# A hybrid decoder block on one core: root of the norms on ScalarE, other loads and order around the second norm

## The chip, the core and the metric

The kernel runs on one core of a Trainium2 chip. Its engines work side by side, each through its own instructions in order: TensorE (PE, matmuls; PEld are its weight loads), VectorE (DVE), ScalarE (ACT), GpSimd (POOL), and SyncE (SP), which here only issues loads. The metric is device time in microseconds (us), the median of several runs; lower is better. All times of the trace count from the first instruction of one profiled execution.

## What is computed

One block for a sequence of 256 positions of width 2048, all in float32 (cut):

```python
mod = silu(c) @ w_mod + b_mod                     # 6 x 2048 columns
sh1, sc1, g1, sh2, sc2, g2 = split(mod, 6)
h = rms_norm(x, norm1_g) * (1 + sc1) + sh1
q, k, v, u, gates = split(h @ w_in)
...                                               # attention, state space branch
x = x + g1 * (merged @ w_out)
h2 = rms_norm(x, norm2_g) * (1 + sc2) + sh2
val, gt = split(causal_dwconv(h2 @ w_up, conv_w, conv_b))
x = x + g2 * ((silu(gt) * val) @ w_down)

def rms_norm(x, g):
    return x * rsqrt(mean(x * x) + EPS) * g
```

## The kernel before

Activations lie with channels on the 128 partitions and the 256 positions along the row. Every weight is streamed once from memory in tiles of 128 x 1024 float32 (512 KB). A float32 product is made of three faster products: ScalarE rounds a weight tile to `whi` (`split_hi`, line 213), VectorE takes the rest, `wlo` = tile - whi (`split_lo`, line 218), and the activations are split in the same way into a pair hi and lo. `raw`, the ring of loaded weight tiles, has five buffers (RAW), `whi` and `wlo` three each (WB); a tile gives its `raw` buffer back when both splits have read it.

The program writes a list, `plan`, of weight tiles and modulation tiles. `go` walks it: `split_ahead(n)` splits up to the tile two behind the current one, `load_ahead` issues loads (line 143, on SyncE's queue) as far as the rings have room, then the tile's matmuls are written. Modulation tiles ("m" entries) are woven between the weights. Two kinds exist: `mod_block` multiplies a tile on TensorE by the conditioning vector (`modp`, line 491, tile matmuls of 512 columns that appear as two records each), copies the sums (`rows`, line 498) and transposes them into columns (`cols_of`, `modt`, line 514); `gate_block` multiplies and sums a tile on VectorE (line 529). After the state space branch the modulation tiles have a ring of their own, `mraw`, with four buffers (MRAW).

A scheduler then fixes the order of the instructions of each engine. It takes the dependencies, the order in which they were written as priority, and its own estimate of when an instruction could start; so a load that waits for nothing can go far ahead of its place in the program. Two devices steer it. `after(a, b)` is an edge that only orders a behind b. And a modulation load into `mraw` is held back by a one-column copy on VectorE from the latest `wlo` into the buffer to be loaded (line 141): the load cannot start before that split.

The stage around the change: the w_out projection (`outp`, blocks b = 0 to 7, 32 weight tiles), whose last block adds each half into x at once (`add_to`, line 356) and squares it on ScalarE (`squares`, line 564; sums over channels by matmuls `sqs`, line 569); `norm_rows(st2)`; the late modulation tiles, the last LATE = 4 units of two tiles each, which give the shift columns 12 to 15 of sh2; then `up_pair(0, 0)`, the first products of w_up (`gp`, then `vp`). `norm_rows` copies the sums, transposes them by two matmuls (`pv`), computes 1/sqrt with a bit trick and three Newton steps on VectorE (`rsqrt`, lines 431 to 435, ten operations on 128 x 2), and spreads the result over all partitions through a diagonal matrix (`dg`) and two matmuls (`pr`) into `rb`. `modulate(c, ...)` then makes the pair `HL[c]`: t = x * a * rb on VectorE (line 603), hi = t + shift on ScalarE (line 607), lo on VectorE (line 608). The first FIRST = 2 pairs are made before the products start, the other six one for each weight step (`spread`). `HL[c]` lies in buffer hl`c`; hl4 to hl7 hold the gated branch (`yg`) until the products `ppp` have read it.

The order of writing here is: w_out's products, `norm_rows`, late tiles, three splits of the next weights (`split_ahead(done["hi"])`), two modulations, then the products. `follow` puts the first weight matmul behind the last modulation matmul.

## Time and profile before

| | |
|---|---|
| runs shown | 1523.32, 1524.7, 1530.68 us; median 1524.7 |
| the profiled execution | 1520.47 us, of which the span from the first to the last instruction is 1518.6 |
| busy | PE 1463.7 us (96%), PEld 1237.9 (82%), DVE 1109.5 (73%), ACT 842.0 (55%), POOL 9.8 (1%) |
| loads | 353.47 MB, mean 233 GB/s |
| mean granted TensorE clock | 0.987 of 2.4 GHz |

Busy times of different engines overlap, so their sum says nothing; what sets the end is the chain of waits. A matmul's row can be longer than the distance to the next one, since they are pipelined: distances between starts are the rate.

### The profile page before, as it was taken

To read this page: it belongs to the slowest core of one execution; us is meant where nothing else is said; L and a number is where in the kernel's file an instruction comes from. 1 tells how busy PE (TensorE), PEld (TensorE's weight loads), DVE (VectorE), ACT (ScalarE), POOL (GpSimd) and SP (SyncE) were. 2 spreads that over 40 slices of the span, in tenths; PEclk is the share of its full clock that TensorE was granted. 3 is DMA by queue.
4 is the path that set the end of the run, shared out by engine and by line. 5 is a ranking of instruction groups with operands and counts; after the bars stand their busy time and mean duration, and the time that the engine had idled before them with its cause. 6 is when DMAs were issued, how large, how long until landed. Compare 5 with 4: busy or idle time off the path is not lost.

```text
span 1518.6 us, 24307 instructions
## 1 busy us (share of the span) xinstructions
PE 1463.7 (96%) x9382; PEld 1237.9 (82%) x9382; DVE 1109.5 (73%) x1881; ACT 842.0 (55%) x1193; POOL 9.8 (1%) x22
## 2 busy tenths in 40 slices
PE   7979999899999999999989999999999999999998
PEld 4657768689977788888868888888888888888887
DVE  3879865886677889998578888886555667766654
ACT  4755767867775534654445555555444455555443
POOL 1000000000000000000000000000000000000000
PEclk9989999999999999999999999999999999999999
DMA  8878888533458887978576777775555555555663
GB/s 322 306 238 307 304 321 296 179 126 126 139 170 298 300 301 276 332 262 315 176 281 235 245 263 262 246 258 191 194 189 188 193 190 186 193 191 186 205 212 107
DMA packets 99109, 353.47 MB, mean 233 GB/s; under 512 B 10961, under 2 KB 13137, under 8 KB 98993
## 3 DMA queue, kind: packets, MB, share of 16 engines
q1 hardware_dynamic: 97808, 348.17, 66.7%
q0 software_dynamic: 1040, 3.61, 0.7%
q8 instruction: 73, 1.20, 0.3%
q14 instruction: 42, 0.34, 0.1%
q10 hardware_dynamic: 146, 0.15, 0.0%
HBM read 349.79 MB, written 2.10 MB: 232 GB/s over the span
## 4 chain that ended last, share of the span: by engine, by line
PE 74%; DVE 10%; DMA 6%; ACT 5%; issue 3%; POOL 0%; SPq 0%; ACTq 0%; DVEq 0%
PE dp L329 11%; PE vp L329 10%; PE gp L329 10%; PE dp L331 6%; PE vp L331 5%; PE gp L331 5%; PE outp L329 4%; DVE wlo L218 4%; ACT whi L213 2%; PE outp L331 2%; PE modp L491 2%; PE ppp L329 2%; PE gap L329 2%; DMA raw<-in_w_m_dram 2%; DMA raw<-in_w_g_dram 2%
## 5 line engine op out<-in xcount | busy, mean ns | idle before, releaser
L218 DVE TENSOR_TENSOR wlo<-raw,whi 128x1024 fp32r<-128x1024 f32 x464 | 566.1, 1222 | 296.6 <-ACT whi L213 294.6
L213 ACT CAST whi<-raw 128x1024 fp32r<-128x1024 f32 x464 | 487.0, 1051 | 521.4 <-PE dp L329 131.8
L329 PE MATMUL vp<-hl,whi 128*128 128x512 f32 x704 | 244.9, 391 | 1.2 <-DVE gate L1307 1.2
L329 PE MATMUL dp<-g,whi 128*128 128x512 f32 x704 | 244.3, 391 | 0.0
L329 PE MATMUL gp<-hl,whi 128*128 128x512 f32 x640 | 222.3, 391 | 0.0
L331 PE MATMUL dp<-g,wlo 128*128 128x256 f32 x704 | 197.7, 281 | 0.0
L331 PE MATMUL vp<-hl,wlo 128*128 128x256 f32 x704 | 197.1, 280 | 0.0
L331 PE MATMUL gp<-hl,wlo 128*128 128x256 f32 x640 | 179.2, 280 | 0.0
L329 PEld LDWEIGHTS vp<-hl,whi 128*128 128x128 f32 x704 | 131.7, 187 | 30.5 <-ACT whi L213 1.5
L329 PEld LDWEIGHTS dp<-g,whi 128*128 128x128 f32 x704 | 131.9, 187 | 28.6
L329 PEld LDWEIGHTS gp<-hl,whi 128*128 128x128 f32 x640 | 119.7, 187 | 26.2
L331 PEld LDWEIGHTS vp<-hl,wlo 128*128 128x128 f32 x704 | 133.1, 189 | 0.0
L331 PEld LDWEIGHTS dp<-g,wlo 128*128 128x128 f32 x704 | 133.0, 189 | 0.0
L331 PEld LDWEIGHTS gp<-hl,wlo 128*128 128x128 f32 x640 | 121.0, 189 | 0.0
L329 PE MATMUL gap<-hl,whi 128*128 128x512 f32 x256 | 92.7, 403 | 0.0
L329 PE MATMUL outp<-m,whi 128*128 128x512 f32 x256 | 90.8, 399 | 0.0
L529 DVE SCALAR_TENSOR_TENSOR raw<-raw,cb 128x1024 f32<-128x1024 f32 x60 | 73.1, 1219 | 22.0 <-DMA raw<-in_w_g_dram 21.5
L529 DVE SCALAR_TENSOR_TENSOR mraw<-mraw,cb 128x1024 f32<-128x1024 f32 x56 | 68.2, 1221 | 17.4 <-DMA mraw<-in_w_g_dram 16.9
L331 PE MATMUL gap<-hl,wlo 128*128 128x256 f32 x256 | 72.2, 282 | 0.5 <-DVE wlo L218 0.5
L331 PE MATMUL outp<-m,wlo 128*128 128x256 f32 x256 | 71.4, 280 | 0.0
L329 PEld LDWEIGHTS gap<-hl,whi 128*128 128x128 f32 x256 | 48.0, 188 | 17.1 <-issue 3.4
L491 PE MATMUL modp<-raw,cpad 128*32 128x512 f32 (+1 forms) x320 | 53.9, 573 | 7.4 <-DMA raw<-in_w_m_dram 6.7
(343 smaller groups left out, 2597.7 us busy)
## 6 DMA issues: line engine op xcount, KB each, us to landing
raw<-in_w_up_dram SPq DMA_DIRECT2D x176, 512.0 KB, 3.6
raw<-in_w_in_dram SPq DMA_DIRECT2D x96, 512.0 KB, 4.8
raw<-in_w_down_dram SPq DMA_DIRECT2D x88, 512.0 KB, 3.5
raw<-in_w_m_dram SPq DMA_DIRECT2D x68, 512.0 KB, 5.1
raw<-in_w_g_dram SPq DMA_DIRECT2D x60, 512.0 KB, 5.1
mraw<-in_w_g_dram SPq DMA_DIRECT2D x56, 512.0 KB, 5.1
raw<-in_w_ga_dram SPq DMA_DIRECT2D x32, 512.0 KB, 4.5
raw<-in_w_out_dram SPq DMA_DIRECT2D x32, 512.0 KB, 4.2
```

Source lines behind the costliest of these rows:

```text
L213: A.copy(hi, loaded[i][0])
L218: V.tensor_sub(lo, loaded[i][0], hi_lo[i][0].bitcast(F32))
L329: follow(PE.matmul(joined(p[m]), hi4[:, k, ms], joined(a), start=u == 0 and k == 0, stop=False, skip_group_check=True))
L331: PE.matmul(p[m][:, 0], lo4[:, k, ms], a[:, 0], start=False, stop=u == kbs - 1 and k == 3, skip_group_check=True)
L491: mm = PE.matmul(st["p"][r0:r0 + 32], cpad[:, k], raw[:, i], start=k < 4, stop=k >= 12, tile_position=(0, r0))
L529: V.scalar_tensor_tensor(flat, flat, 1.0, cb[:, 1024 * half:1024 * half + 1024], op0=ALU.mult, op1=ALU.mult, accum_out=sums[:, k, half:hal ...
```

## The change

Norm: `norm_rows` no longer calls `rsqrt`. ScalarE computes the root of pv/(32 D) + EPS straight from the bank (`AF.Sqrt` with a bias tile `eps`), VectorE the reciprocal and one Newton step, three operations. A first `AF.Sqrt` of `eps` is ordered behind the last square. The copy of `a1` into `dg`, which held the first norm back behind the modulation scale, is dropped.

Loads: while `place["norm"]` is set (from the second norm to the first two modulations), modulation loads are not held back. The first half of the late tiles (two units, four tiles) is loaded by four transfers written behind block b = 3 of the w_out projection, into hl4 to hl7; their matmuls are written directly behind the norm. The other four tiles pass through `mraw` as before.

Third split: `split_ahead(done["hi"] - 1)` leaves the third weight tile to the first step of `go`, and its `wlo` is ordered behind the last operation of the second modulation (`behind["h"]`).

```diff
--- before.py
+++ after.py
@@ -137,7 +137,7 @@
         held[r] += 1
         raw = ring[r]()
 
-        if r == "mod" and "lo" in place:
+        if r == "mod" and "lo" in place and not place.get("norm"):
             V.tensor_copy(raw[:, 0, 0:1], place["lo"][:, 0, 0:1].bitcast(F32))
         flat = raw.rearrange("p a b -> p (a b)")
         DMA.dma_start(flat, src)
@@ -215,7 +215,9 @@
 
     def split_lo(i):
         lo = wp.tile([128, 2, 512], F32R, name="wlo", tag="wlo", bufs=WB)
-        V.tensor_sub(lo, loaded[i][0], hi_lo[i][0].bitcast(F32))
+        split = V.tensor_sub(lo, loaded[i][0], hi_lo[i][0].bitcast(F32))
+        if "h" in behind:
+            after(split, behind.pop("h"))
         hi_lo[i][1] = lo
         place["lo"] = lo
         unload(i)
@@ -561,7 +563,7 @@
         if ks[0] == 0:
             st["p"] = py_tile([128, 256], "sqs")
         sq = w4("sq", (128, len(ks), 256))
-        A.activation(sq, src, AF.Square)
+        st["sq"] = A.activation(sq, src, AF.Square)
 
         def add():
             for i, k in enumerate(ks):
@@ -574,22 +576,27 @@
         else:
             add()
 
-    def norm_rows(st, after=None):
-
+    def norm_rows(st):
+
+        eps = sm.tile([128, 2], F32, name="eps", tag="mx")
+        G.memset(eps, EPS)
         v2 = sm.tile([128, 2], F32, name="v2", tag="v2", bufs=1)
         r2 = sm.tile([128, 2], F32, name="r2", tag="r2", bufs=1)
         t2 = sm.tile([128, 2], F32, name="t2", tag="t2", bufs=1)
+        after(A.activation(t2, eps, AF.Sqrt), st["sq"])
         sqs = w4("sqs", (128, 256))
         V.tensor_copy(sqs, st["p"])
         pv = py_tile([128, 2], "pv")
         for t in range(2):
             PE.matmul(pv[:, t:t + 1], sqs[:, 128 * t:128 * t + 128], ones[:, 0:1], start=True, stop=True)
+        A.activation(t2, pv, AF.Sqrt, scale=1.0 / (32 * D), bias=eps[:, 0:1])
         V.tensor_scalar(v2, pv, 1.0 / (32 * D), EPS, op0=ALU.mult, op1=ALU.add)
-        rsqrt(r2, v2, t2)
+        V.reciprocal(r2, t2)
+        V.scalar_tensor_tensor(t2, r2, -0.5, r2, op0=ALU.mult, op1=ALU.mult)
+        V.tensor_mul(t2, t2, v2)
+        V.scalar_tensor_tensor(r2, t2, 1.5, r2, op0=ALU.add, op1=ALU.mult)
         pr = py_tile([128, 256], "pr")
         dg = w4("dg", (128, 2, 128))
-        if after is not None:
-            V.tensor_copy(dg[:, 0, 0:1], after)
         for t in range(2):
             V.tensor_scalar(dg[:, t], ident, r2[:, t:t + 1], None, op0=ALU.mult)
             PE.matmul(pr[:, 128 * t:128 * t + 128], ones, dg[:, t], start=True, stop=True)
@@ -605,8 +612,8 @@
         for i in range(2):
             k = 2 * c + i
             A.activation(HL[c][:, i, 0], t[:, i], AF.Identity, bias=sh[:, k:k + 1])
-            V.scalar_tensor_tensor(HL[c][:, i, 1], t[:, i], sh[:, k:k + 1], HL[c][:, i, 0].bitcast(F32),
-                                   op0=ALU.add, op1=ALU.subtract)
+            place["h"] = V.scalar_tensor_tensor(HL[c][:, i, 1], t[:, i], sh[:, k:k + 1],
+                                                HL[c][:, i, 0].bitcast(F32), op0=ALU.add, op1=ALU.subtract)
 
     def make_h(k0, nk):
         for c in range(k0 // 2, (k0 + nk) // 2):
@@ -1053,7 +1060,7 @@
     st1 = {}
     for q in range(8):
         squares(st1, range(2 * q, 2 * q + 2), xT[q])
-    norm_rows(st1, a1[:, 0:1])
+    norm_rows(st1)
     mods += m0[len(m0) // 2:]
     all_mods()
     go()
@@ -1285,11 +1292,20 @@
                                       lambda p, ms, b=b: out_post(b, p, ms), groups=b == 7), R_OUT)
         if b % 2:
             go()
+        if b == 3:
+
+            early = [part for unit in late[:LATE // 2] for part in unit]
+            there = [pair(8 - LATE + i, "late", F32) for i in range(LATE)]
+            for (src, _, _), raw in zip(early, there):
+                DMA.dma_start(raw.rearrange("p a b n -> p (a b n)"), src)
     all_mods()
     go()
     flush()
+    place["norm"] = True
     norm_rows(st2)
-    mods += late
+    for (_, fn, _), raw in zip(early, there):
+        fn(raw.rearrange("p a b n -> p a (b n)"))
+    mods += late[LATE // 2:]
     all_mods()
     go()
 
@@ -1352,7 +1368,7 @@
                                           lambda p, ms, i=i: val_post(j, n, i, p)), R_FFN)
 
     up_pair(0, 0)
-    split_ahead(done["hi"])
+    split_ahead(done["hi"] - 1)
 
     def modulate2(cs):
         for c in cs:
@@ -1360,6 +1376,8 @@
             yield 1
 
     drain(modulate2(range(FIRST)))
+    place["norm"] = False
+    behind["h"] = place["h"]
     spread(modulate2(range(FIRST, 8)), 1.0, True)
 
     for hf, (j0, j1) in enumerate(((0, 6), (6, 11))):
```

## Rows read from the trace of the kernel before

**Rows 1.** The page: its part 1 (busy time, share of the span and instructions of each engine) and, from part 2, the busy share of PE in 40 equal slices of the span of 38 us each, in tenths.

```profile
PE 1463.7 (96%) x9382; PEld 1237.9 (82%) x9382; DVE 1109.5 (73%) x1881; ACT 842.0 (55%) x1193; POOL 9.8 (1%) x22
...
PE   7979999899999999999989999999999999999998
```

**Rows 2.** The chain of waits between 755 and 815 us, the links around the second norm: start, us, what.

```profile
769.69 1.23 DVE wlo L218
...
772.66 0.30 DVE dg L594
...
776.25 0.15 DVE mraw L141
```

**Rows 3.** The timeline of TensorE (PE) from 760 to 782 us: start, us, engine, line, operation, out<-in, count, and in brackets the idle time before with its releaser.

```profile
766.00 0.59 PE L491 MATMUL modp<-mraw,cpad 128*32 128x512 f32 x1 [1.25 <-issue]
...
768.34 1.06 PE L491 MATMUL modp<-mraw,cpad 128*32 128x512 f32 x6
771.18 1.02 PE L491 MATMUL modp<-mraw,cpad 128*32 128x512 f32 x2 [1.78 <-DVE t L434]
...
774.21 3.10 PE L491 MATMUL modp<-mraw,cpad 128*32 128x512 f32 x14
777.39 0.39 PE L295 MATMUL gp<-hl,whi 128*128 128x256 f32 x1
...
779.84 0.66 PE L514 MATMUL modt<-p,rows 128*128 128x128 f32 x4 [0.91 <-ACT rows L498]
780.25 0.36 PE L295 MATMUL gp<-hl,whi 128*128 128x256 f32 x1
```

**Rows 4.** The timeline of SyncE's DMA queue (SPq) from 744 to 822 us: start, time from the first to the last issue of the row, what is loaded, how many.

```profile
758.19 2.00 SPq L143 DMA_DIRECT2D mraw<-in_w_m_dram  x4
...
767.66 2.75 SPq L143 DMA_DIRECT2D mraw<-in_w_m_dram  x4
```

**Rows 5.** The timeline of VectorE (DVE) from 744 to 822 us.

```profile
764.79 1.00 DVE L356 SCALAR_TENSOR_TENSOR x<-outp,g,x 128x256 f32<-128x256 f32 x2 [0.38 <-PE outp L331]
...
768.45 0.16 DVE L587 TENSOR_SCALAR v<-pv 128x2 f32<-128x2 f32 x1 [0.39 <-PE pv L586]
769.42 0.23 DVE L141 COPY mraw<-wlo 128x1 f32<-128x1 f32 x2 [0.82 <-PE modp L491]
...
770.83 0.15 DVE L433 SCALAR_TENSOR_TENSOR t<-r 128x2 f32<-128x2 f32 x1
...
774.32 0.42 DVE L596 COPY rb<-pr 128x256 f32<-128x256 f32 x1 [1.18 <-PE pr L595]
776.17 0.23 DVE L141 COPY mraw<-wlo 128x1 f32<-128x1 f32 x2 [1.42 <-PE modp L491]
```

**Rows 6.** Three stretches from views by windows: stretch, its length, busy time and instructions of PE, PEld, DVE, ACT and POOL, granted TensorE clock (1.00 is 2.4 GHz, 0.50 is 1.2 GHz), share of the 16 DMA engines, GB/s.

```profile
26.00:30.00 4.00, 3.41 (x15) 3.12 (x16) 4.00 (x8) 2.17 (x3) 0.00 (x0) 0.50 0.90 300
...
773.00:774.00 1.00, 0.91 (x4) 0.93 (x4) 0.14 (x1) 0.00 (x0) 0.00 (x0) 0.50 0.95 377
...
776.00:800.00 24.00, 22.75 (x185) 21.29 (x180) 23.83 (x53) 13.98 (x24) 0.00 (x0) 1.00 0.76 264
```

**Rows 7.** The timeline of all engines from 14 to 31 us, the first norm: the first and the last of VectorE's ten small operations with what follows them, and the matmuls of pr.

```profile
20.27 0.17 DVE L431 TENSOR_SCALAR r<-v 128x2 int32<-128x2 int32 x1
...
22.24 0.48 DVE L594 TENSOR_SCALAR dg<-p,r 128x128 f32<-128x128 f32 x2
...
22.67 0.68 PE L595 MATMUL pr<-dg,ones 128*128 128x128 f32 x4 [1.63 <-DVE dg L594]
```

**Rows 8.** The timeline of ScalarE (ACT) over several stretches: table loads, the first activation that computes Sin on 32 columns, the last squares of the second norm and the first modulation behind it.

```profile
3.96 1.28 ACT L420 ACT_TABLE_LOAD   x1 [3.96 <-DMA p<-in_p_dram]
...
89.86 0.23 ACT L455 ACTIVATE scr<-scr 128x32 f32<-128x32 f32 x1 [2.43 <-DVE scr L674]
...
301.79 1.28 ACT L874 ACT_TABLE_LOAD   x1
...
765.62 0.72 ACT L564 ACTIVATE sq<-x 128x256 f32<-128x256 f32 x2
...
776.83 1.31 ACT L607 ACTIVATE hl<-t,sh 128x256 fp32r<-128x256 f32 x3 [10.49 <-DVE t L603]
...
815.29 1.28 ACT L1341 ACT_TABLE_LOAD   x1 [0.16 <-DVE gate L1307]
816.58 1.06 ACT L1341 ACTIVATE gate<-gate 128x1024 f32<-128x1024 f32 x1
```

**Rows 9.** Groups by line and shape, VectorE: the reciprocal of the attention (busy us, mean ns of one, idle before).

```profile
L991 DVE RECIPROCAL l<-l 128x2 f32<-128x2 f32 x8 | 1.3, 162 | 5.5 <-ACT e L988 5.3
```

**Rows 10.** Two stretches of the w_out stage by windows, columns as in rows 6.

```profile
680.00:690.00 10.00, 10.00 (x59) 8.22 (x59) 9.20 (x18) 4.83 (x6) 0.00 (x0) 1.00 1.02 419
...
700.00:710.00 10.00, 10.00 (x58) 8.16 (x57) 9.86 (x17) 3.73 (x4) 0.00 (x0) 1.00 0.93 364
```

**Rows 11.** Timelines of the w_out stage, one row each of TensorE's weight loads, ScalarE and VectorE.

```profile
692.83 0.19 PEld L331 LDWEIGHTS outp<-m,wlo 128*128 128x128 f32 x1 [0.27 <-DVE wlo L218]
...
706.90 1.05 ACT L213 CAST whi<-raw 128x1024 fp32r<-128x1024 f32 x1 [1.36 <-DMA raw<-in_w_out_dram]
...
706.95 1.22 DVE L529 SCALAR_TENSOR_TENSOR mraw<-mraw,cb 128x1024 f32<-128x1024 f32 x1
```

**Rows 12.** The timeline of TensorE from 814 to 818 us.

```profile
815.36 0.47 PE L329 MATMUL vp<-hl,whi 128*128 128x512 f32 x1 [1.24 <-DVE gate L1307]
```

## The prediction

> **What bounds the kernel now.** I read the page first. TensorE is busy 1463.7 of 1518.6 us, so only stretches in which it is idle, or runs at its lower clock, can give time back [rows 1]. Of the 40 slices five are under nine tenths: the first, the third, the eighth, the last, and the 21st, 759 to 797, which holds the second norm [rows 1].
>
> The chain of waits says what the 21st is: behind the w_out projection it leaves TensorE for VectorE, and two of the links there do no arithmetic for the norm, the third split (1.23 us) and a one-column hold copy [rows 2]. TensorE's own timeline closes the picture: the projection ends 1.25 us before 766.00, and the first late matmul must wait until VectorE has read its bank (764.79 + 1.00); gp starts at 777.39, stops for the transposed shift columns (modt, 779.84), and runs without a gap from 780.25 [rows 3, 5]. In these 15.5 us, from 764.75 to 780.25, the reader should see three things.
>
> First, the late modulation matmuls come in two lots. Records 1 to 16 are done by about 769.4; the next two wait until 771.18, and 14 more run from 774.21, behind pr [rows 3]. The queue shows why: four tiles are requested at 758.19 and the other four only from 767.66, when the first four give their buffers back [rows 4]. Second, VectorE's queue: the norm's v is ready at 768.45 + 0.16, but two hold copies stand in front of the root until about 769.6 (769.42 + 0.15), the split takes VectorE from 769.69 to 770.83, and after pr two hold copies wait for the late matmuls until 776.17, with the modulation behind them [rows 2, 5]. Third, with TensorE idle from 769.4 to 771.18 the granted clock fell to 0.50 at 773, that is to 1.2 GHz [rows 6]; the late records cost 3.10/14 = 0.22 us there against 1.06/6 = 0.18 before [rows 3].
>
> **The change, part by part.** My sum is a new time line of this stretch at the second norm, then three smaller terms.
>
> *Root on ScalarE.* Before, v and ten small VectorE operations run in a row. At the first norm that is 20.27 to 22.24, one start every 0.197 us [rows 7]. After, ScalarE takes the root from the bank, and reciprocal plus three operations follow. No Sqrt row exists; the nearest small activation took 0.23 us, a 128x2 reciprocal 0.16 us [rows 8, 9]. So 0.23 + 0.04 + 4 x 0.197 = 1.06 us instead of 0.19 + 1.97 = 2.16: a gain of 1.1 us at each norm. Bounds for the root: 0.16, as the reciprocal, and 0.36, half of the last two squares' 0.72 [rows 9, 8].
>
> *Table loads.* Sqrt needs another table set. A table load took 1.28 us, and the next activation started 0.01 us after it [rows 8]. The dummy root behind the last square puts the load at 766.34 to 767.62 at the second norm [rows 8]; the dummy itself ends at 767.85, ahead of the bank's 768.4 [rows 5], so it is hidden by the pv matmuls and costs up to 1.3 us if the scheduler puts it later. Behind it on ScalarE nothing is due before the modulation, 10.49 us later [rows 8]. No load appears between 3.96 and 301.79, although Sin runs at 89.86: Sin lives in the set loaded for Silu [rows 8]. After Sqrt has replaced it, Sin needs a load of its own; this one has no designed cover. Bounds 0 and 1.28; I take 0.9. The first norm is thus worth -1.1 + 0.9 = -0.2 us.
>
> The Trainium skill (ScalarE: Activation LUTs, "What ACT_TABLE_LOAD costs") charges 2.66 us for a switch, 1.28 for the load and 1.38 for a drain. The trace agrees on the load and shows no drain behind it [rows 8]. By the page the dummy root would end 1.4 us later, after pv, and the sum would be worse by about 1 us here and by up to 1.4 us at Sin.
>
> *Holds and third split.* Removing the holds gives back 768.61 to 769.6 in front of the root and the wait before 776.17 [rows 5]; moving the split gives 1.1 us [rows 2, 5]. Its ScalarE half (whi) lies in or before ScalarE's 10.49 us of idle time and costs nothing [rows 8]. The order edge holds only the VectorE half, behind the eighth modulation operation; its reader is gp's third weight tile. Together with the root, dg moves from 772.66 [rows 2] to 768.45 + 1.06 = 769.5.
>
> *Early loads and late matmuls.* All eight late tiles can now be in place at 766.0: four in hl4 to hl7, free since the ppp matmuls, four in the modulation ring, idle once the last gate product there has run (706.95 + 1.22) [rows 11]. TensorE still cannot begin before the projection's bank is free. Sixteen records with sqs and pv end at 769.4 as before; pr then has the first half of dg (0.3 us) at 769.8 and takes 0.68 us at the full clock (first norm's row) [rows 7], to 770.5; 16 records of 0.177 us end at 773.3. Behind pr stand rb (0.42 us), one t (some 0.45) and one hl (1.31/3 = 0.44), as before [rows 5, 8]: the first hl is there at about 772.0, so gp starts at 773.3 instead of 777.39: 4.1 us. From there to 780.25 TensorE did 0.7 us of gp and 0.66 of modt and lost about 1.5 us [rows 3]; with hl ready ahead I take a loss of 0.6. **Second norm: -5.0 us.** Bounds: all 32 records ahead of pr gives 2.4; no loss at modt gives 5.9.
>
> *What the loads displace.* No byte is added, but eight tiles of 512 KB, on SP's queue, move forward in time with nothing to pace them. SP issues whatever is ready, so they go out as soon as their buffers are free: four at about 667 to 671, four at 701 to 708. They stand in front of w_out weights. A tile costs 1.25 us at the 419 GB/s of 680 to 690 [rows 10]. That stretch and 700 to 710 are already nearly full [rows 10], and cover is thin: TensorE waited 0.27 us for a split at 692.83, and ScalarE 1.36 us for a weight at 706.90 [rows 11]. Bounds: 0, and 8 x 1.25 = 10.0 us. Between the lots the queue has room, and the weight ring is five deep, so I take 1.5.
>
> *Downstream.* VectorE is busy 23.83 of 24 us after the norm [rows 6]. It gets the split (1.14 us) in this stretch and loses some holds. TensorE waits 1.24 us at 815.36 for the first gate's convolution at the end of this backlog [rows 12]. Bounds: -1.2 (wait gone) and +1.1 (split added whole); I take +0.5.
>
> *At nothing:* the memset of eps, POOL being busy 1% of the span [rows 1]; the dropped a1 copy (0.14 us or less, off the chain); the early matmuls' hold on hl4 to hl7, over by 773, before the third modulation pair. Uncovered, each is a few tenths.
>
> Sum: -5.0 - 0.2 + 1.5 + 0.5 = **-3.2 us**. The profiled execution took 1520.47 us, 1.9 more than its span, so it would take 1517.3. That execution lies 4.2 us under the median of the runs shown, 1524.7; against that median the same sum gives **1521.5 us**, which is the forecast.
>
> **The rivals.**
>
> *The preload starves w_out* (the other side). Place: 680 to 715. Each tile that really goes ahead of a due weight costs 1.25 us; above 4.7 us of TensorE wait, four of the eight tiles, the kernel is slower than before. For it: the two waits above and the 1.02 DMA share [rows 10, 11]. Against it: the five-deep ring. With six tiles on the path, 7.5 us: 1524.7 - 4.7 + 7.5 = 1527.5. With all eight, 1530.
>
> *Full clock at both norms.* TensorE's granted clock is 0.50 from 26 to 30, after similar idle spots at the first norm [rows 6]. Were the shorter chain to keep 2.4 GHz, half of some 6.5 us of matmul time, 3.3 us, is saved; with no loss in the w_out stage: -5.9 - 3.5 = -9.4, 1515.3. Against it: only 1.1 of the first norm's idle time goes.
>
> *The gain is handed back at the gate.* VectorE, not TensorE, sets the time up to 815. Then its earlier start counts, t at about 771.5 instead of 776.4, 4.9 us, less the split and one gate product (1.22 us, as the row at 706.95 [rows 11]) that an unheld load brings forward into this stretch: 2.5. With the other terms, 1524.7 - 2.5 - 0.2 + 1.5 = 1523.5. For it: 23.83 of 24 [rows 6]. Against it: gp has no gap after 780.25 [rows 3].
>
> *The loads of tables are on the path.* Three loads of 1.28 us (two roots, Sin) [rows 8] cost 3.8 us where the sum has 0.9: it leaves -0.3, 1524.4. For it: nothing but the scheduler's order keeps the dummy root ahead of pv. Against it: ScalarE has nothing else to do there. The Trainium skill (ScalarE: Activation LUTs, "Table sets: the hidden batching unit") advises to batch activations by set, against which this change goes.
>
> **How the numbers follow.** Forecast 0.55, its own range 1518.5 to 1524; preload starves 0.15; gate 0.14; full clock 0.10; table loads 0.06. The range 1515 to 1528.5 reaches into both outer rivals and takes in the runs' own scatter. Half a per cent, 7.6 us, is about what a measurement of this kernel can tell from no change. Faster by more needs the full-clock case with little lost: 0.09. Slower by more needs more than the eight tiles' whole price or the last part of that rival: 0.04. Within: 0.87.
>
> **What would show it.** In the profile of the changed kernel: Sqrt between pv and the reciprocal, its load ended before; dg some 1.1 us after pv; no wlo between them; 32 modp records without a DMA wait and the clock at 1.00 throughout; gp some 8.6 us after the last outp matmul instead of 12.6; a load of tables at Sin. A TensorE wait for wlo or whi between 680 and 715 would show the preload's price, a longer wait at the first gate the downstream one. The prediction is wrong if the late matmuls are ordered before pr, if the preload's waits exceed 5 us, or if the first norm's low clock goes away.

## The result, and the profile after

The changed kernel took 1513.23 us (median of 9 runs, 1508.01 to 1516.53) beside 1523.32 us for the kernel before (9 runs, 1513.10 to 1530.68): a ratio of 0.9946 with a 95% interval of 0.9924 to 0.9967, that is -8.2 us (-11.6 to -5.0). A second measurement of the same kernel (experiment 7) gave 1513.99 against 1522.03 us, ratio 0.9967 (0.9946 to 0.9988). The profiled execution took 1514.07 us, span 1512.3 us, 6.3 less than before.

The page of the changed kernel, TensorE's line of part 1 and its 40 slices. The 21st slice has gone from 8 to 9 tenths or more [rows 1]:

```profile
PE 1461.0 (97%) x9382; PEld 1235.3 (82%) x9382; DVE 1106.5 (73%) x1859; ACT 846.8 (56%) x1200; POOL 9.9 (1%) x24
...
PE   8979999899999999999999999999999999999998
```

The timeline of the changed kernel: TensorE from the first late matmul to the first value matmul after the convolution's wait, then VectorE, then ScalarE, each in order of time (start, us, engine, line, operation, out<-in, count, idle before and its releaser). Line numbers are two higher than before from 220 on, five to seven higher in the norm and the modulation, and sixteen higher in the up projection.

```profile
763.41 0.59 PE L493 MATMUL modp<-late,cpad 128*32 128x512 f32 x1 [1.14 <-issue]
...
766.33 1.45 PE L493 MATMUL modp<-mraw,cpad 128*32 128x512 f32 x9
767.71 0.71 PE L602 MATMUL pr<-dg,ones 128*128 128x128 f32 x4
768.35 1.06 PE L493 MATMUL modp<-mraw,cpad 128*32 128x512 f32 x6
770.13 0.66 PE L516 MATMUL modt<-p,rows 128*128 128x128 f32 x4 [0.72 <-ACT rows L500]
770.54 0.38 PE L297 MATMUL gp<-hl,whi 128*128 128x256 f32 x1
771.91 0.39 PE L299 MATMUL gp<-hl,whi 128*128 128x256 f32 x1 [0.99 <-DVE hl L615]
...
809.00 0.47 PE L331 MATMUL vp<-hl,whi 128*128 128x512 f32 x1 [1.13 <-ACT whi L213]
...
766.32 0.16 DVE L593 TENSOR_SCALAR v<-pv 128x2 f32<-128x2 f32 x1 [1.32 <-ACT t L592]
...
767.17 0.48 DVE L601 TENSOR_SCALAR dg<-p,r 128x128 f32<-128x128 f32 x2
...
770.82 0.18 DVE L517 TENSOR_REDUCE sh<-modt 128x4 f32<-128x16 f32 x1 [1.02 <-PE modt L516]
...
803.14 1.22 DVE L531 SCALAR_TENSOR_TENSOR mraw<-mraw,cb 128x1024 f32<-128x1024 f32 x1 [1.08 <-DMA mraw<-in_w_g_dram]
...
71.61 1.28 ACT L457 ACT_TABLE_LOAD   x1
72.91 0.31 ACT L457 ACTIVATE scr<-scr 128x128 f32<-128x128 f32 x1
...
763.88 1.28 ACT L586 ACT_TABLE_LOAD   x1
765.17 0.20 ACT L586 ACTIVATE t<-eps 128x2 f32<-128x2 f32 x1
766.02 0.26 ACT L592 ACTIVATE t<-pv,eps 128x2 f32<-128x2 f32 x1 [0.65 <-PE pv L591]
```

The late matmuls now run in one stream, 26 of the 32 records ahead of pr (767.71) and six behind it, without a wait for a transfer; before, two of the second lot ran at 771.18 and 14 behind pr [rows 3]. dg follows v by 0.85 us. Then a new wait shows: VectorE stops 1.02 us at the reduction of the late shift columns, and TensorE 0.99 us behind it.

SyncE's queue in the changed kernel: the early loads, one at 663.47 and three from 700.17 on, then the first and the last of the four late tiles that pass through `mraw`.

```profile
663.47 0.33 SPq L1300 DMA_DIRECT2D late<-in_w_m_dram  x1
...
700.17 2.49 SPq L1300 DMA_DIRECT2D late<-in_w_m_dram  x3
...
722.63 0.43 SPq L143 DMA_DIRECT2D mraw<-in_w_m_dram  x1
...
734.68 0.42 SPq L143 DMA_DIRECT2D mraw<-in_w_m_dram  x1
```

Windows of the changed kernel, columns as in [rows 6]: in this execution TensorE keeps 1.00 where before it fell to 0.50, and VectorE is busy without a pause from 772 on.

```profile
772.00:774.00 2.00, 2.00 (x17) 2.00 (x18) 2.00 (x6) 1.02 (x2) 0.00 (x0) 1.00 0.00 0
774.00:776.00 2.00, 2.00 (x19) 2.00 (x19) 2.00 (x7) 1.13 (x2) 0.00 (x0) 1.00 0.04 4
776.00:800.00 24.00, 23.13 (x181) 22.26 (x180) 24.00 (x45) 13.24 (x20) 0.00 (x0) 1.00 0.78 275
```

**Where the time went.** Fourteen profiled executions stand behind this document. I cut each into three: the head, to the start of the last outp matmul; the norm's stretch, from there to the 20th cast of an up weight on ScalarE (whi); and the tail. Inside the stretch two marks are given, the first gp matmul and the first vp matmul (us after the last outp matmul). "low" says that the granted clock fell to 0.50 in the norm's stretch: in the kernel before and in experiment 1 at pr and the late matmuls, ahead of gp, for some 3 and 6 us; in the other four behind gp's first matmuls, for some 3 us.

```
kernel                        head    gp     vp          stretch  tail   span
before                        764.5  12.92  38.18 low    70.5    683.6  1518.6
before, again (e12)           766.5  13.01  36.79        73.2    687.9  1527.6
root at first norm (e1)       763.1  13.31  38.17 low    73.6    683.6  1520.3
root at second norm (e2)      762.1  13.04  36.61        68.7    687.9  1518.7
changed, no preload (e4)      758.7  12.91  36.47        68.4    687.9  1515.0
preload alone (e10)           761.0   9.74  33.84        65.8    687.9  1514.7
changed, old roots (e3)       758.2   9.22  34.47        66.4    687.9  1512.5
changed                       762.0   8.55  34.40        66.6    683.7  1512.3
changed, again (e7)           761.8   8.56  35.92 low    68.0    687.9  1517.7
changed, first root old (e9)  758.0   8.55  35.88 low    67.9    687.9  1513.7
changed, holds kept (e6)      760.5   9.11  36.44 low    68.0    683.6  1512.2
changed, early split (e5)     758.2   9.20  35.06 low    67.0    687.9  1513.2
changed, late reduction (e8)  763.4   8.56  33.72        65.3    683.6  1512.3
e5 and e8, copies later (e11) 759.5   8.55  32.55        64.7    687.9  1512.1
```

The stretch is what the change shortens: 72.4 us on average in the three executions with the second norm as before, 67.5 us in the three as changed, -4.9 us. Of this 2.3 us are won by the first vp matmul (37.7 to 35.4, two of three low on both sides) and 2.6 us behind it (34.7 to 32.1). The first part is there in every pair at the same clock: 2.4 us between the two executions that stayed at 1.00 (36.79 to 34.40), 2.3 us between those that fell. The second is not: the first executions of the two kernels took 32.3 and 32.2 us behind vp, and the mean comes from experiments 12 and 1 (36.4 and 35.4 us), to which experiment 12 returns. The tail takes one of two lengths, 683.6 or 687.9 us, in either kernel, and the head scatters by 8 us; that is the scatter of the runs.

### The profile page after: what moved, and what is told of

It is laid out like the page before. It is cut to its first block, busy times and chain, and to the rows that moved or that the text cites. A ratio compares the mean times of both kernels' runs of the same rounds, so it can differ in the third digit from the quotient of the medians.

```text
span 1512.3 us, 24290 instructions
## 1 busy us (share of the span) xinstructions
PE 1461.0 (97%) x9382; PEld 1235.3 (82%) x9382; DVE 1106.5 (73%) x1859; ACT 846.8 (56%) x1200; POOL 9.9 (1%) x24
## 4 chain that ended last, share of the span: by engine, by line
PE 76%; DVE 9%; DMA 7%; ACT 5%; issue 3%; SPq 0%; POOL 0%; ACTq 0%; DVEq 0%
PE vp L331 11%; PE dp L331 11%; PE gp L331 10%; PE dp L333 6%; PE vp L333 5%; PE gp L333 5%; PE outp L331 4%; DVE wlo L218 3%; DMA raw<-in_w_m_dram 2%; PE modp L493 2%; PE gap L331 2%; PE outp L333 2%; ACT whi L213 2%; PE ppp L331 2%; DMA raw<-in_w_in_dram 2%
```

## The experiments

All ratios are to the kernel before on the same chip.

**1. The new root at the first norm alone** (norm_new is the function of the changed kernel, norm_old the former one).

```diff
-    norm_rows(st1, a1[:, 0:1])
+    norm_new(st1)
...
-    norm_rows(st2)
+    norm_old(st2)
```

> The kernel before with the new root at the first norm alone (the copy of a1 into dg dropped too); the second norm keeps its bit trick, holds, split and loads. Theory A (what the second norm does not explain comes from the first norm, whose shorter chain and shorter stretch at the low clock last): 2 to 4 us faster than before, ratio 0.9975 to 0.9985, and the gain is still there at 300 us. Theory B (the first norm gives nothing that lasts: the load of tables at Sin and the loads that feed the first stage take it back; the 4 us beyond the second norm are variation between runs in the first 300 us): ratio 0.9995 to 1.0005.

1519.87 us against 1521.47, ratio 0.9996 (0.998 to 1.0013): the time shows nothing, as theory B has it. The trace does: in the eight executions with the new root the first up matmul started 6.85 to 6.86 us behind the start of the last square-sum matmul of the first norm, in the six with the old one 7.38 to 8.60 us. (The expectations of experiments 9 and 12 count from merged rows and are up to 0.1 us longer.)

**2. The new root at the second norm alone.**

```diff
-    norm_rows(st1, a1[:, 0:1])
+    norm_old(st1, a1[:, 0:1])
...
-    norm_rows(st2)
+    norm_new(st2)
```

> The kernel before with the new root at the second norm alone; holds, early split and late loads stay. By the chain of before, the root saves 1.1 us in front of dg, but the holds and the split stand in VectorE's queue as before and the second lot of late tiles is still requested from 767.7 on, so gp's start is still set by the last late matmul. Theory A: 0 to 0.5 us faster (the second lot of late matmuls sets gp). Rival: the whole 1.1 us shows in the distance from the last outp matmul to gp, 11.5 us instead of 12.6.

1517.51 us, ratio 0.9973 (0.9954 to 0.9992). Its TensorE timeline at the norm:

```profile
769.48 0.68 PE L600 MATMUL pr<-dg,ones 128*128 128x128 f32 x4 [2.45 <-DVE dg L599]
...
771.43 1.05 PE L491 MATMUL modp<-mraw,cpad 128*32 128x512 f32 x4 [0.28 <-DMA mraw<-in_w_m_dram]
...
774.17 1.05 PE L491 MATMUL modp<-mraw,cpad 128*32 128x512 f32 x4 [0.24 <-DMA mraw<-in_w_m_dram]
775.15 0.38 PE L295 MATMUL gp<-hl,whi 128*128 128x256 f32 x1
```

pr is 1.2 us earlier than before, 7.37 us behind the last outp matmul instead of 8.62, but gp is not (13.04): the second lot of late matmuls, which waits for transfers, is queued ahead of it. What the root frees is lost there. The 4 us that the time shows (1.2 to 7.0 by the interval) would then lie behind the norm: from vp to the 20th cast it took 32.1 us, where the kernel before takes 32.3 to 36.4 (experiment 12). That these are the same microseconds is argued, not shown.

**3. The change with the old roots at both norms.**

```diff
-    norm_rows(st1)
+    norm_old(st1, a1[:, 0:1])
...
-    norm_rows(st2)
+    norm_old(st2)
```

> The changed kernel with the old bit trick at both norms: no holds, later third split, early loads. Theory A (the second norm's gain is mostly the late tiles that are there in time and the holds; the first norm's root gives the rest of the whole): 3 to 4 us faster than before, ratio 0.9972 to 0.998, no gain in the first 300 us. Theory B (the second norm is all there is, the rest is variation): the same as the whole change within its interval, 0.994 to 0.9965. In both gp starts about 1 us later behind the last outp matmul than in the changed kernel.

1517.08 us, ratio 0.9976 (0.9961 to 0.9991): theory A's ratio, though the interval just touches theory B's. gp is 0.7 us later than in the changed kernel (9.22), not 1. vp comes at 34.47 us, as in the changed kernel (34.40): with the preload there, the second root is worth 0.7 us at gp and nothing at vp.

**4. The change without the early loads** (all eight late tiles are loaded behind the w_out weights, unheld).

```diff
-        if b == 3:
...
-                DMA.dma_start(raw.rearrange("p a b n -> p (a b n)"), src)
...
-    for (_, fn, _), raw in zip(early, there):
-        fn(raw.rearrange("p a b n -> p a (b n)"))
-    mods += late[LATE // 2:]
+    mods += late
```

> The changed kernel without the early loads: all eight late tiles pass through the modulation ring of four buffers, not held back. If the early loads are what lets the late matmuls run in one stretch, the last four tiles are requested only when the first four have been used, some 5 us later, and gp starts 2 to 3 us later than in the changed kernel, with the clock at 0.50 again. Rival: four tiles without a hold are enough, since the ring refills while pv, root and pr run: 0 to 1 us later.

1516.16 us, ratio 0.997 (0.9954 to 0.9986). The TensorE timeline:

```profile
767.81 1.05 PE L493 MATMUL modp<-mraw,cpad 128*32 128x512 f32 x4 [1.47 <-DMA mraw<-in_w_m_dram]
...
771.62 0.39 PE L297 MATMUL gp<-hl,whi 128*128 128x256 f32 x1
```

Root, unheld loads and later split together leave gp at 12.91 and vp at 36.47 us, beside 13.01 and 36.79 us in the kernel before at the same clock: next to nothing without the preload. gp is 4.4 us later than in the changed kernel, more than the 2 to 3 us expected, and the clock stayed at 1.00, against the expectation.

**5. The change with the early third split.**

```diff
-    split_ahead(done["hi"] - 1)
+    split_ahead(done["hi"])
...
-    behind["h"] = place["h"]
```

> The changed kernel with the third weight tile of the up block split as early as the kernel before does it, all else as changed. Theory A (VectorE's idle stretches in the norm, 1.26 us ahead of the sums' copy and 1.32 us ahead of the first scaling in the changed kernel's trace, can take the 1.22 us of the split): the first up matmul stays at its place within 0.3 us, and the split is gone from the row of modulations behind it, so that the up block's later waits on VectorE shrink: 0 to -1.2 us against the changed kernel. Theory B (the split falls into the norm's chain on VectorE, as it did in the kernel with the new root alone, where it stood between the reciprocal and the next operation): the reciprocal's chain, and with it the first up matmul, come up to 1.2 us later, and no later wait pays it back: 0 to +1.2 us. The trace tells them apart by the place of the split and the first up matmul's offset; the time hardly can.

1513.41 us against 1522.03, ratio 0.9955 (0.9933 to 0.9978). The split falls into VectorE's idle time, as theory A had it; but the held copies of the gate tiles, no longer behind a late split, slip in front of dg and delay gp by 0.65 us:

```profile
759.52 1.23 DVE L218 TENSOR_TENSOR wlo<-raw,whi 128x1024 fp32r<-128x1024 f32 x1
...
764.11 0.15 DVE L141 COPY mraw<-wlo 128x1 f32<-128x1 f32 x1 [0.72 <-PE modp L493]
```

Even so vp comes at 35.06 us with a low clock, against 35.92 in experiment 7: the later split costs 0.9 us here.

**6. The change with the held loads kept.**

```diff
-    place["norm"] = True
```

> The changed kernel with the held-back loads kept around the second norm: each of the four late modulation tiles that are still loaded there, and the gate tiles behind them, wait for the latest low half of a weight tile, as before. Theory A (the loads held back were part of the stall, as the prediction has it): the four tiles are issued behind VectorE's split and land up to 2 us later, the one-element copies of 0.2 us stand in VectorE's row between the norm's operations, and the first up matmul is 1 to 2.5 us later than in the changed kernel: +1 to +2.5 us. Theory B (with half of the tiles loaded beforehand the other half have time enough): the second lot of late matmuls still ends before the modulated activations are there; the first up matmul moves by less than 0.5 us: 0 to +0.5 us.

1513.84 us, ratio 0.9956 (0.9931 to 0.9982); gp 0.55 us and vp 0.52 us later than in experiment 7, both low. Theory B, nearly: dropping the holds is worth half a microsecond once half of the tiles are there.

**7. The changed kernel again,** no edit.

> The changed kernel itself, unchanged, beside its parts on one chip. Theory A (the sum of what the trace shows at the second norm is all there is, and the rest of the first measured difference was the spread of few runs): 3.5 to 5 us below the kernel before, ratio 0.9967 to 0.9977. Theory B (something of the change outside the second norm gains too, which the parts run so far do not show): 7 to 9 us below, ratio 0.994 to 0.9955. The row of TensorE's 64-matmul weight tiles between 832 and 1054 us is read as well: 2.773 us each or 2.827 us each, which makes 4 us over some 75 tiles.

1513.99 us, ratio 0.9967 (0.9946 to 0.9988), wide enough for both theories. But this execution fell differently from the first. Windows of it, to be set against those of the first execution above:

```profile
772.00:774.00 2.00, 2.00 (x13) 2.00 (x13) 2.00 (x6) 1.02 (x2) 0.00 (x0) 0.65 0.00 0
774.00:776.00 2.00, 2.00 (x12) 2.00 (x11) 1.79 (x6) 0.00 (x0) 0.00 (x0) 0.50 0.10 23
```

With the same program, the same waits (0.99 us ahead of it) and the same start of gp the clock fell, and vp came 1.5 us later. And in the tail each 128x512 matmul took 5 ns more at a granted clock of 1.00. The groups by line between 832 and 1054 us, of the first execution and then of this one:

```profile
L331 PE MATMUL vp<-hl,whi 128*128 128x512 f32 x320 | 111.2, 394 | 0.0
```

```profile
L331 PE MATMUL vp<-hl,whi 128*128 128x512 f32 x320 | 113.3, 399 | 0.0
```

**8. The change with the late shift reduction one tile later.**

```diff
-    ...cols_of(rows, 3, 4 * j, 4, sh2), bu_tile, lag)
+    ...cols_of(rows, 3, 4 * j, 4, sh2), bu_tile, lag or (j == 3))
```

> The changed kernel, with the last reduction of the late shift tiles (VectorE, columns 12 to 15, needed only by the seventh and eighth pairs of modulated tiles) put one weight tile later than the third modulation instead of ahead of it. In the changed kernel VectorE waits 1.02 us there for the late transposes, and TensorE 0.99 us behind it for the first low half. Theory A (VectorE is what bounds the stretch from the second norm to the end of the modulations, so an idle microsecond of it is worth one): TensorE's wait of 0.99 us at the first low half shrinks to 0.2 us or less, the later waits of 0.33 and 0.54 us do not grow, and the time falls by 0.8 to 1.3 us against the changed kernel. Theory B (the weight splits that follow set the pace and the microsecond comes back as waits on VectorE or ScalarE): TensorE's waits behind 775 us grow by what the first one shrank, and the time is the changed kernel's within 0.3 us.

1513.71 us, ratio 0.9962 (0.9937 to 0.9988). The 1.02 us wait on VectorE is gone; a shorter one takes its place:

```profile
770.32 1.28 DVE L610 SCALAR_TENSOR_TENSOR t<-x,a,rb 128x256 f32<-128x256 f32 x3
771.92 0.88 DVE L615 SCALAR_TENSOR_TENSOR hl<-t,sh,hl 128x256 fp32r<-128x256 f32 x2 [0.32 <-ACT hl L614]
```

vp comes at 33.72 instead of 34.40 us: 0.7 us, what VectorE's idle time shrank by, a little under theory A's range; of TensorE's two later waits behind VectorE one grew from 0.33 to 0.48 us. The time cannot tell it.

**9. The change with the old root at the first norm alone.**

```diff
-    norm_rows(st1)
+    norm_old(st1, a1[:, 0:1])
```

> The changed kernel with the shift-and-Newton inverse root and its held copy put back at the first norm alone, all else as changed. Ten profiled executions so far: from the last square sum of the first norm to the first up-projection matmul the three with the old root took 7.44, 8.21 and 8.66 us, the seven with the new one 6.90 to 6.99 us, and the 60th matmul of that stretch came at 17.18 to 18.11 us against 14.47 to 17.12 us. Theory A (the first norm's shorter chain is kept: it spares 0.5 to 1.8 us of stall and about half of the low-clock stretch behind it): the first up matmul is 0.5 to 1.8 us later than 6.90 us, and the time 1.5 to 2.5 us above the changed kernel's. Theory B (the gain is given back where the sine's table is now loaded a second time, or in the loads behind): the same delay at the first up matmul, but a time within 1 us of the changed kernel's.

1518.52 us against 1521.36, ratio 0.9977 (0.9952 to 1.0001). The first up matmul came 8.19 us behind the last square sum, 1.3 us later than with the new root. Its window of the clock behind that, and the same window of experiment 7 and of the changed kernel's first execution:

```profile
26.00:30.00 4.00, 2.59 (x9) 1.89 (x10) 3.27 (x7) 3.66 (x5) 0.00 (x0) 0.50 0.83 292
```

```profile
26.00:30.00 4.00, 3.28 (x31) 3.00 (x31) 4.00 (x8) 2.08 (x3) 0.28 (x1) 1.00 0.90 326
```

```profile
26.00:30.00 4.00, 3.22 (x16) 3.18 (x16) 4.00 (x8) 1.98 (x3) 0.18 (x1) 0.59 0.92 346
```

The clock is not always whole with the new root, but it is always higher: 0.59 to 1.00 from 26 to 30 us in the eight executions with it, 0.50 to 0.55 in the six with the old one. From the last square sum to the first `gep` matmul, a stage further on at some 55 us, the eight took 35.8 us on average (34.5 to 36.6), the six 37.4 (36.4 to 39.0): 1.6 us are still there. By the ratios theory A is favoured, but the intervals overlap, and this execution's head, 758.0 us, is the shortest of all. Over all heads the new root has 760.9 us on average (eight, 758.2 to 763.4), the old one 761.7 (six, 758.0 to 766.5); in their scatter 1.6 us do not show. What the first norm is worth at the end of the kernel stays open, between nothing and some 2 us.

**10. The preload alone,** in the kernel before: old roots, holds, early split.

```diff
+        if b == 3:
+
+            early = [part for unit in late[:LATE // 2] for part in unit]
+            there = [pair(8 - LATE + i, "late", F32) for i in range(LATE)]
+            for (src, _, _), raw in zip(early, there):
+                DMA.dma_start(raw.rearrange("p a b n -> p (a b n)"), src)
...
-    mods += late
+    for (_, fn, _), raw in zip(early, there):
+        fn(raw.rearrange("p a b n -> p a (b n)"))
+    mods += late[LATE // 2:]
```

> The kernel before with one part of the change alone: half of the late modulation tiles loaded ahead, in the output block. Old roots, held-back loads and the early third split stay. From the last output matmul to the first value matmul of the up block the profiled executions took 38.18 and 38.17 us with nothing changed there (both with a low-clock stretch, worth 1.5 us, at the first gate matmuls), 36.61 us with the new root alone, 36.47 us with everything but the preload, 34.47 us with everything but the roots, 34.40 us with all, 35.92 us with all and a low-clock stretch. Theory A (the preload is what gains, since the late matmuls bound the stretch and the root, the holds and the split only matter once it is there): 34.4 to 35.3 us at full clock or 1.5 us more with a low stretch, and 2 to 4 us below the kernel before. Theory B (the root's chain and the holds are in the way again as soon as the tiles are there): 36 us or more at full clock, and less than 2 us below the kernel before.

1514.39 us, ratio 0.9952 (0.9927 to 0.9977): as much as the whole change. Its TensorE timeline:

```profile
765.37 2.30 PE L491 MATMUL modp<-mraw,cpad 128*32 128x512 f32 x15
768.46 0.68 PE L595 MATMUL pr<-dg,ones 128*128 128x128 f32 x4 [0.79 <-DVE dg L594]
...
770.77 0.38 PE L295 MATMUL gp<-hl,whi 128*128 128x256 f32 x1 [1.20 <-ACT hl L607]
```

All the late matmuls stand ahead of pr, in the time in which TensorE would wait for the old root anyway; gp then waits only for the modulated tile. vp at 33.84 us beats the changed kernel's 34.40. Theory A, and more than its range on both counts.

**11. Early split, held copies and shift reduction put later, in the changed kernel.**

```diff
-            V.tensor_copy(raw[:, 0, 0:1], place["lo"][:, 0, 0:1].bitcast(F32))
+            hold = V.tensor_copy(raw[:, 0, 0:1], place["lo"][:, 0, 0:1].bitcast(F32)); "hold" in behind and after(hold, behind["hold"])
...
-    ...cols_of(rows, 3, 4 * j, 4, sh2), bu_tile, lag)
+    ...cols_of(rows, 3, 4 * j, 4, sh2), bu_tile, lag or (j == 3))
...
-    split_ahead(done["hi"] - 1)
+    split_ahead(done["hi"])
...
-    behind["h"] = place["h"]
+    behind["hold"] = place["h"]
```

> The changed kernel with three changes of order around its second norm: the third weight tile split early again, as in the kernel before; the one-element copies that hold back the gate tiles put behind the second pair of modulated tiles; and the late shift tiles' reduction put one weight tile later. From the last output matmul to the first value matmul the early split alone took 35.06 us with a low-clock stretch (about 33.6 us without), with the held copies in front of the norm's next operation for 0.72 and 0.55 us; the later reduction alone took 33.72 us against 34.40 us. Theory A (VectorE is the bound from the second norm to the end of the modulations, so what is taken out of its row there adds up): 32.0 to 33.2 us at full clock, 1.2 to 2.4 us below the changed kernel. Theory B (the weight splits on ScalarE, which wait for TensorE to free their buffers, take over): 33.4 us or more, within 1 us of the changed kernel.

1510.68 us, ratio 0.9935 (0.991 to 0.9959), the lowest of all, though its interval overlaps the changed kernel's. The VectorE timeline has the split ahead of the sums, and nothing foreign up to the first three modulations:

```profile
760.80 1.23 DVE L218 TENSOR_TENSOR wlo<-raw,whi 128x1024 fp32r<-128x1024 f32 x1
...
764.70 0.48 DVE L601 TENSOR_SCALAR dg<-p,r 128x128 f32<-128x128 f32 x2
...
766.45 1.28 DVE L610 SCALAR_TENSOR_TENSOR t<-x,a,rb 128x256 f32<-128x256 f32 x3
```

vp at 32.55 us, 1.85 us below the changed kernel at full clock: theory A. The parts about add up: 0.7 us of experiment 8 and 0.9 us of experiment 5, which still had the copies in its way. The copies alone were not run.

**12. The kernel before, again,** no edit, one execution.

> The kernel before once more, unchanged, for a second profiled execution. Theory A (the low-clock stretch at the second norm and the rate of 2.773 or 2.827 us per weight tile between 832 and 1054 us belong to the execution, not to the kernel): one or both may come out differently from the first profiled execution (low at 772 us, 2.773 us); the stretch from the last output matmul to the first value matmul is 38.2 us with the low stretch, 36.7 us without, and the first up matmul of the first norm comes 7.4 to 8.7 us behind the last square sum. Theory B (they belong to the kernel): both as in the first execution.

1529.67 us, span 1527.6. Theory A: no low clock this time (vp 36.79), and the long tail. TensorE's wait ahead of pr and the windows of the clock behind it:

```profile
773.30 1.02 PE L491 MATMUL modp<-mraw,cpad 128*32 128x512 f32 x2 [1.90 <-DVE t L434]
```

```profile
772.00:774.00 2.00, 0.70 (x2) 0.14 (x2) 1.79 (x8) 0.00 (x0) 0.00 (x0) 1.00 0.84 279
774.00:776.00 2.00, 1.23 (x8) 0.67 (x10) 1.15 (x6) 0.00 (x0) 0.00 (x0) 1.00 0.94 360
```

The stretch is nevertheless 2.7 us longer than in the first execution, for what comes behind vp. The timeline, SyncE's queue, VectorE and TensorE:

```profile
804.25 1.27 SPq L143 DMA_DIRECT2D mraw<-in_w_g_dram  x1
...
812.32 1.23 DVE L529 SCALAR_TENSOR_TENSOR mraw<-mraw,cb 128x1024 f32<-128x1024 f32 x1 [3.45 <-DMA mraw<-in_w_g_dram]
...
818.17 0.51 PE L329 MATMUL vp<-hl,whi 128*128 128x512 f32 x1 [3.45 <-DVE gate L1307]
```

The sixth gate tile behind the norm is late. VectorE waits 3.45 us for it, and behind that fused product in its queue stand the first gate's convolution and the weight splits; TensorE loses as much at vp. In the first execution the same TensorE wait was 1.24 us [rows 12], in experiment 1 it was 2.80 us. The tile is requested 37.8 to 39.2 us behind the last outp matmul in these three; with the preload alone at 34.6, in the changed kernel at 35.2 and 36.7, without the preload but unheld at 36.6, and with the new root alone at 36.6 us. In none of the eleven executions with a part of the change at the second norm does it take more than 32.2 us from vp to the 20th cast, where those three took 32.3, 36.4 and 35.4. Part of this is the transfer itself: 8.0 and 7.4 us from issue to landing here and in experiment 1, 5.8 and 5.9 us in the first executions of the two kernels. The issue alone took 0.97 to 1.52 us in the three executions with the second norm as before, 0.33 to 0.40 us in the eleven others. Why it took longer is open, and so is how often it does; two late tiles in three executions are few.

## Why the prediction was right and wrong

I forecast 1521.5 us, a gain of 3.2 us against the 1524.7 of three runs; by the ratios it was 8.2 us in one measurement and 5.0 in the other. The median of 1513.23 lies below the range; the first ratio on the forecast's own base, 1524.7, gives 1516.5, which lies inside. Of the 8.3 us between forecast and median 1.4 to 3.3 us are the base: more runs put the kernel before at 1521.4 to 1523.3. The rest is terms.

**The second norm, -5.0.** Much of the new time line was right: the table load hidden (763.88 to 765.16, the bank at 766.02), 32 late records without a transfer's wait, and gp 8.55 us behind the start of the last outp matmul, where it was drawn at 773.3, that is 8.8 us on this count (the 8.6 of the signs counts from that matmul's end). That gp came out so close is partly luck. 26 records, not 16, went ahead of pr, and the last record ended 7.4 us behind the last outp matmul (769.41), 1.4 us sooner than drawn; then TensorE waited 0.72 us for the copied sums and ran the transposes (modt) ahead of gp, where they were drawn behind it. Late matmuls ahead of pr were named as a sign of being wrong; in experiment 10 all 32 are, and vp comes 0.6 us sooner than in the changed kernel. Of the bounds, 5.9 does not follow: with no loss at modt the terms give 4.1 + 1.5 = 5.6. The step that failed is what follows gp: I allowed 0.6 us for the transposed columns. TensorE lost 0.99 us at the first low half and 0.33 and 0.54 us at later ones, all behind VectorE, so that of 4.4 us at gp 2.3 are left at vp (4.5 and 2.4 in the pair at full clock). The kernel before lost 0.26 and 0.91 us there in its first execution, behind the low clock [rows 3], and nothing in experiment 12. I had read VectorE's 23.83 of 24 us and set it at nothing but +0.5, because gp had no gap after 780.25 [rows 3, 6]. A queue that is nearly full, though it leaves no gap downstream yet, takes back what is won ahead of it.

**Which part does it.** My sum gave the root 1.1 us, the holds and the split about as much each, and the preload the rest. Experiments 2, 4 and 10 show these not to be additive: without the preload the late matmuls bound gp and the other parts give 0.2 to 0.3 us at vp (36.61 and 36.47 beside 36.79); with it they give half a microsecond (holds), 0.7 us at gp and nothing at vp (root), and the later split loses about 0.9 us.

**Downstream, +0.5, bounds -1.2 to +1.1.** Wrong in sign and outside its bounds on average, -2.6 us; in the first executions of the two kernels nothing, 32.3 and 32.2 us, so the size hangs on the two late tiles of experiments 1 and 12. I took the wait of 1.24 us at 815.36 for VectorE's backlog [rows 12]. It was a gate tile's transfer, 3.45 us in another execution, and the change requests that tile some 2.5 us earlier at the same state of the clock. VectorE's own wait, 6 us ahead of it, names the DMA. The line of the kernel before:

```profile
809.50 1.23 DVE L529 SCALAR_TENSOR_TENSOR mraw<-mraw,cb 128x1024 f32<-128x1024 f32 x1 [1.24 <-DMA mraw<-in_w_g_dram]
```

The rival that hands the gain back at the gate had the place right and the direction wrong.

**The preload's price, +1.5, bounds 0 to 10.** Some tenths. From its first to its last outp matmul the w_out stage took 95.6 us on average with the preload (nine, 94.8 to 96.5) and 95.3 without (five, 94.9 to 95.7). Between 680 and 715 TensorE's weight loads waited for a split 0.7 us on average with the preload, 0.4 us without. The longest such wait is that of experiment 8, where 1.08 us of it reached the matmuls:

```profile
709.47 0.19 PEld L333 LDWEIGHTS outp<-m,wlo 128*128 128x128 f32 x1 [1.40 <-DVE wlo L218]
```

Against the kernel before, the cast at 711.6 us of the changed kernel's first execution came 3.5 us later than that at 664.1 did, and by 734.8 they were level again: the five-deep ring took it. The loads also did not go out as the term had it. One of the early four was issued at 663.47 and three from 700.17 on, not four at 667 to 671; the four through `mraw` followed one by one from 722.63 to 734.68, not at 701 to 708. So only three of the eight tiles were issued between 680 and 715, where the rival that starves w_out has them, and that rival falls.

**The first norm, -0.2.** Too small, by what the traces show: 1.6 us are won by the first `gep` matmul (experiment 9), through the shorter chain (0.5 to 1.8 us at the first up matmul) and the higher clock behind it. The load at Sin shows, at 71.61 us; Sin first runs at 71.52 in the kernel before, not at 89.86. Its 0.9 us are not seen: from the first `gep` matmul to the first of the next stage (`zp`) the eight executions with this load took 161.8 us on average, the six without it 162.5, with a scatter of over 1 us. The Trainium skill (ScalarE: Activation LUTs, "What ACT_TABLE_LOAD costs") adds 1.38 us of drain to the 1.28 us of a load. The traces show the load and, both at 72.91 and at 765.17, an activation 0.01 to 0.02 us behind it, and the load itself 0.01 to 0.02 us behind the end of the activation before it; the measurement decides.

**The clock.** I tied the low clock at 773 to TensorE's idle time before it, 1.78 us [rows 3]. In experiment 12 TensorE idled 1.90 us at the same place, in experiment 2 2.45 us ahead of pr, and the clock stayed at 1.00. At the second norm it fell in six executions of fourteen, and in one of the two of each kernel, before and changed; so the change does not decide it. Between executions of one kernel a fall is worth 1.4 to 1.5 us at vp. At the first norm the new root does raise it (0.59 to 1.00 beside 0.50 to 0.55). The full-clock rival is right in part: the clock behind the first norm was whole in two of the eight executions with the new root, experiments 5 and 7.

## What to carry to other kernels

When a stretch has several late things, find the one that ends last at the consumer before pricing the others: here four transfers moved forward did alone what the whole change did, and the other parts were worth something only behind them. Follow a wait through every queue to its last link; "waits for VectorE" was a transfer two links back. And compare stretches between marks in the traces, not whole times, when single effects are a microsecond and the runs scatter by ten; but count the executions, since a mean of three can hang on one late transfer.

## What the runs showed of the hardware

- The granted clock at one place fell to 0.50 in one execution and stayed at 1.00 in another of the same program, with the same instructions and waits ahead of it.
- TensorE has two rates at a granted clock of 1.00 in the up stage, 394 and 399 ns per 128x512 matmul between 832 and 1054 us, in different executions of one program. From the 20th cast to the first matmul of the down projection that is 213.4 or 217.5 us, nearly all of the difference between the tails of 683.6 and 687.9 us. What chooses between them stays open.
- The gate tile of 512 KB that VectorE waited for took 8.0 us from its issue to its landing in experiment 12, while the four weight tiles issued from 800 to 815 us took 4.9 us (median).
